# A gated hybrid decoder layer in split fp32: one planner orders everything from the second projection pass to w_o, the pooled branch moves ahead of the gates, five column pairs there use seven-product blocks, and convolution taps alternate between two tiles

## The chip, the core and the metric

The kernel runs on one core of a Trainium2 chip. The metric is the device time of one execution in microseconds (us). Three runs of the kernel before gave 1199.72, 1199.89 and 1200.82 us; their median is 1199.89.

Engines: TensorE (PE, with PEld for its weight loads) multiplies, VectorE (DVE) and ScalarE (ACT) do elementwise work, GpSimd (POOL) and SyncE (SP) here mostly start DMAs.

## The reference

272 tokens (16 meta tokens and a sequence of 256) of width 2048, one layer:

```python
u = rms_norm(h, g_pre_mix)
z_pool, v_conv, g_conv, gate_a, gate_b = split(u @ w_in)      # 1024 | 1024 | 1024 | 2048 | 2048
y_a = causal_multiscale_pool(z_pool, w_pool_grp, pool_scale) @ w_pool_out
y_b = conformer_conv(v_conv, g_conv, w_dw, b_dw, ...) @ w_conv_out
m = sigmoid(gate_a) * y_a + sigmoid(gate_b) * y_b
h = h + rms_norm(m @ w_o, g_post_mix)
h = h + rms_norm(square(relu(rms_norm(h, g_pre_mlp) @ w_up)) @ w_down, g_post_mlp)
return h[:, 16:]
```

The pool takes trailing means over 2, 4, 8 and 16 tokens in four channel groups, subtracts the token, and maps each group by a 256x256 matrix. The convolution multiplies v by sigmoid(g), applies 31 causal taps per channel, a LayerNorm over channels and a swish. Everything is fp32.

## The kernel before

**Split weights.** Each fp32 factor of a product is held as two fp32r parts, hi (rounded) and lo (the rest), and a product is three matmuls: hi·hi, lo·hi and hi·lo. Weights come in chunks of 128x2048 fp32 (1 MB), loaded by SP into one of three buffers `raw`. `open_chunk` (L300) makes the load and two instructions: ACT copies raw to hi (L319), DVE subtracts, lo = raw − hi (L322). Hi and lo each have three rooms in turn, so the split of a chunk can start when the chunk three places earlier has been multiplied. `fetch` (L339) hands out a chunk and issues the split of the one two ahead.

**Stages, in PE's order.** The first convolution pass v0; then g0, v1, g1, v2, g2, v3, g3 and z0 to z3, each a projection of 256 columns with features on partitions and 272 tokens in the free dimension (`project`, matmuls L497); 16 blocks of 512 columns for the two gates (`project_t`, matmuls L753, output tokens x columns; a chunk of 512 input features makes a product of 12 matmuls for each of the two token tiles, 2.72 us each, and a block has four chunks); the pool's group map (`acc_grp`, L497); w_pool_out (`acc_po`), w_conv_out (`acc_co`) and w_o (`acc_o`), four blocks each; and the MLP.

**What orders the other engines there.** Emission is in program order, and each engine runs its instructions in that order. `project` and `project_t` emit a matmul group, then take a given amount of small work (`fill`, in us of DVE) from a list `pending` by `drain`. The list holds the 240 convolution taps (`conv_tile`, L559 to L567: c = a·tap + c on 128x256, one channel tile after the other, 30 in a row for a tile, DVE L563), the pool's running sums (L673 to L685), and the LayerNorm steps (L698 to L731). Evacuations stand between them: L570, L577, L650 for the projections, L854, L882, L883 for the branches.

**The planner.** The MLP part of the kernel is ordered by a class `Plan` (L32 to L163). Each piece of work is added with its engine, a cost and what it reads and writes. PE's row is fixed by hand; each other piece gets a due time from the PE piece that needs it; a small simulation with the costs then always takes the ready piece that is due first, and the resulting start times give the order of emission. In the MLP the planner also orders "seven-product blocks": a 2x2x2 block product (two chunks of features by two column blocks by two token tiles) is done with seven products instead of eight, from sums of weight blocks and of activation blocks ("forms"). A weight sum is either a DVE addition on raw chunks (L1211), or a second load that POOL starts and that accumulates into the raw chunk (L1216).

Of the kernel before, what the change touches and what calls it, by code (L numbers as in the profile page):

```python
# [16 lines left out]
P = 128  # L17
CK = 4
# [12 lines left out]

class Plan:  # L32
# [5 lines left out]
    def __init__(self):  # L38
        self.work = []
        self.writer = {}  # L40
        self.readers = {}

    def add(self, engine, cost, f, reads=(), writes=(), late=0.0):
        i = len(self.work)
        before = set()
        for b in reads:
            if b in self.writer:
                before.add(self.writer[b])
        for b in writes:
            before.update(self.readers.get(b, ()))  # L50
            if b in self.writer:
                before.add(self.writer[b])
        for b in reads:
            self.readers.setdefault(b, []).append(i)
        for b in writes:
            self.writer[b] = i
            self.readers[b] = []
        before.discard(i)
        self.work.append((engine, cost, f, sorted(before), late))
# [107 lines left out]
def hybrid_block(ctx: ExitStack, tc: tile.TileContext, ins: dict, out: bass.AP):  # L167
# [88 lines left out]
    for h in range(CC // HALF_CW):  # L256
        for c0 in (PW, PW + CC):
            stream += columns(w_in, 0, KD, c0 + h * HALF_CW, HALF)
    for h in range(PW // HALF_CW):
        stream += columns(w_in, 0, KD, h * HALF_CW, HALF)  # L260
    standing_chunks = set()
    for n in range(2 * D // CW):
        stream += columns(w_in, 0, KD, G0 + n * CW)
    stream.append((w_grp.rearrange("g (k p) c -> p (g k) c", p=P), (NG * GD // P, GD)))
    for w, nk in ((w_pool_out, KP), (w_conv_out, KC)):
        for n in range(NB):
            stream += columns(w, 0, nk, n * CW)
    for n in range(NB):
        stream += columns(w_o, 0, KD, n * CW)

    spare = {len(stream) + 1: "s0", len(stream) + 2: "s1"}
    PF = 2 * CW
    NP = FF // PF
    standing_chunks.update(range(len(stream), len(stream) + NB + 2))
    stream += columns(w_up, 0, KD, 0)
    stream += columns(w_up, 0, KD, CW, HALF)
    FIRST = KD // HALF[0]
    opened = []
    at = {"n": 0}
# [3 lines left out]
    PLACES = {n: (2, 1) for n in standing_chunks}  # L283
# [16 lines left out]
    def open_chunk():  # L300
        n = at["n"]
        at["n"] += 1
        src, (rows, width) = stream[n]
# [4 lines left out]
        else:  # L308
            hi, lo = part_tile("hi", n), part_tile("lo", n)
# [158 lines left out]
    def scale_roots():  # L468
        tot = tmp.tile([P, NT + 1], F32, tag="tot", name="tot0")
        nc.vector.reduce_sum(tot, ssq, axis=mybir.AxisListType.X)  # L470
        nc.vector.tensor_scalar(tot, tot, 1.0 / D, RMS_EPS, op0=ALU.mult, op1=ALU.add)
        sc["r"] = r = const.tile([P, NT + 1], F32, name="r_in")
        q = tmp.tile([P, NT + 1], F32, tag="rs", bufs=1, name="rs_q_in")
        nc.scalar.activation(q, tot, AF.Sqrt)
        warm_up(AF.Sigmoid)
        rsqrt(r, q, tot)
        sc["diag"] = []
        for t in range(NT + 1):
            n = P if t < NT else M
            dg = tmp.tile([P, P], F32, tag="v", bufs=5, name=f"diag_{t}")  # L480
            nc.vector.tensor_scalar_mul(dg[:n, :n], ident[:n, :n], r[:n, t:t + 1])
            sc["diag"].append(dg)

    def scale_rows():
        pb = misc_tile("pb")
        for t, lo_, n in [(NT, 0, M)] + [(t, M + t * P, P) for t in range(NT)]:
            nc.tensor.matmul(pb[:, lo_:lo_ + n], ones[:n, :], sc["diag"][t][:n, :n],
                             start=True, stop=True)
        nc.vector.tensor_copy(rb, pb[:, :L])


# [28 lines left out]
    def project(act, nk, evac, name, mm=mm2, width=CW, shape=HALF, fill=0.0):  # L520

        ck, cw = shape
        accs = [acc[:, :width] for acc in acc_tiles(name, cw // P)]
        for kc in range(nk // ck):
            hi, lo = fetch()
            for j, acc in enumerate(accs):
                for k in range(ck):
                    kk = kc * ck + k
                    mm(acc, hi, lo, act, (k, kk), slice(j * P, (j + 1) * P), kk == 0, kk == nk - 1)
                if kc == nk // ck - 1:  # L530
                    flush(1)
                    evac(j, acc)
                if fill:
                    drain(fill * P / cw)

    def halves(acc, name):

        t = tmp.tile([P, T], F32, tag="v", bufs=5, name=f"half_{name}")
        nc.scalar.copy(t, acc[:, :T])
        s = tmp.tile([P, T], F32, tag="v", bufs=5, name=f"sum_{name}")  # L540
        nc.vector.tensor_add(s, t, acc[:, T:])
        return s

    def split(dst, k, src):
        def f():
            nc.scalar.copy(dst[:, k, 0, :], src)
            nc.vector.tensor_sub(dst[:, k, 1, :], src, f32(dst[:, k, 0, :]))
        late.append(f)


# [3 lines left out]

    def conv_tile(q):
        def first():
            nc.scalar.activation(conv["c"][:, q, :], conv["a"][:, q, 0:T], AF.Identity,
                                 scale=taps[:, q, 0:1], bias=col("b_dw", q))

        def tap(i):  # L560
            def f():
                c = conv["c"][:, q, :]
                nc.vector.scalar_tensor_tensor(c, conv["a"][:, q, i:i + T], taps[:, q, i:i + 1],  # L563
                                               c, op0=ALU.mult, op1=ALU.add)
            return f
        return [(0, first)] + [(0.39, tap(i)) for i in range(1, TAPS)]

    def evac_v(j, acc):
        v = tmp.tile([P, L], F32, tag="v", bufs=5, name=f"v_{j}")
        nc.vector.tensor_mul(v, acc[:, :L], rb)  # L570
        gv.append(v)

    def evac_g(j0):
        def f(j, acc):
            q = j0 + j
            g = tmp.tile([P, L], F32, tag="g", name=f"g_{q}")
            nc.vector.tensor_mul(g, acc[:, :L], rb)  # L577

            def gated():
                nc.scalar.activation(g, g, AF.Sigmoid)  # L580
                nc.vector.tensor_mul(conv["a"][:, q, PAD:], gv.pop(0), g)
                pending.extend(conv_tile(q))
            late.append(gated)
        return f

# [11 lines left out]
    accs = [acc[:, :L] for acc in acc_tiles("v0", HALF_CW // P)]  # L597
# [15 lines left out]
    def after_first():  # L613
        scale_rows()
        for j, acc in enumerate(accs):
            evac_v(j, acc)

    def tap_columns():
        rows_to_columns(*other_rows)
        pt = misc_tile("taps_t")  # L620
        for q in range(KC):
            nc.tensor.transpose(pt[:, q * 32:q * 32 + TAPS], taps_in[:, q * P:(q + 1) * P],
                                ident[:TAPS, :TAPS])
# [1000 lines left out]
```

## Time and profile before

| | |
|---|---|
| three runs | 1199.72, 1199.89, 1200.82 us |
| the profiled execution | 1200.3 us, of which 1198.5 us is the span from the first to the last instruction |
| granted TensorE clock, mean | 0.997 |
| busy in the span | PE 99%, PEld 86%, DVE 85%, ACT 55%, POOL 3% |
| DMA | 270.80 MB, 226 GB/s on average |

How to read it: "busy" is the time in which an engine runs instructions. PE's matmuls overlap, so the mean of one matmul in a list (390 ns) is longer than the distance from one to the next. A row of the view by windows gives, for a stretch of the span, the busy time of PE, PEld, DVE, ACT and POOL with the count of instructions in brackets, then the granted clock, the DMA share and GB/s. In this execution v0 ends and g0 begins at about 28.8 us, the gates run from 161 to 336, the group map to 342.6, w_pool_out to 386, w_conv_out to about 437, w_o to about 520 and the MLP to 1187.

### The profile page before, as it was taken

Reading aid. Unit: us, or ns where it says so; the run is one execution under the profiler, and the core shown is the slowest. Engines: PE = TensorE matmul, PEld = TensorE weight load, DVE = VectorE, ACT = ScalarE, POOL = GpSimd, SP = SyncE. Lnnn points to the kernel's source line nnn. Section 1 sums busy time; section 2 is a strip of 40 time slices with the busy share of each in tenths; the row PEclk is TensorE's granted clock in tenths of the full one; section 3 lists DMA queues with packets and bytes.
Section 4 is the critical chain, followed back from the end, with each engine's and each line's share of the span. In section 5 each row is a group of like instructions: output and inputs, shape, how many; then the busy total and the mean of one; then the engine's idle time right before and its main releaser. Section 6 shows DMA issues by size and latency. Waiting matters only on the chain.

```text
span 1198.5 us, 15727 instructions
## 1 busy us (share of the span) xinstructions
PE 1184.1 (99%) x6384; PEld 1026.1 (86%) x6384; DVE 1013.4 (85%) x1084; ACT 661.4 (55%) x664; POOL 41.7 (3%) x45
## 2 busy tenths in 40 slices
PE   9999999999999999999999999999999999999996
PEld 8999988888888888898888888888888888888885
DVE  5799987999767664577989999999999999899856
ACT  6633334434475334357676665666665756666542
POOL 1000000000000000000100000000000000000000
PEclk9999999999999999999999999999999999999998
DMA  8655555656556756549998897997997987979941
GB/s 257 210 178 180 179 191 187 198 189 201 185 176 212 280 176 201 186 123 354 245 332 231 236 314 203 243 319 189 289 293 199 309 236 240 316 179 263 332 139 71
DMA packets 176698, 270.80 MB, mean 226 GB/s; under 512 B 4482, under 2 KB 91970, under 8 KB 175713
## 3 DMA queue, kind: packets, MB, share of 16 engines
q1 hardware_dynamic: 160064, 235.09, 58.6%
q0 software_dynamic: 15408, 32.66, 15.1%
q10 hardware_dynamic: 1152, 2.04, 0.5%
q8 instruction: 50, 0.82, 0.3%
q14 instruction: 24, 0.19, 0.0%
HBM read 265.58 MB, written 4.19 MB: 225 GB/s over the span
## 4 chain that ended last, share of the span: by engine, by line
PE 98%; DMA 1%; DVE 1%; ACT 0%; ACTq 0%; issue 0%; DVEq 0%
PE bank_u L502 18%; PE acc_gate L753 15%; PE acc_up L1373 13%; PE bank_u L508 9%; PE bank_a L1373 7%; PE bank_b L1373 5%; PE acc_o L753 5%; PE acc_v L497 4%; PE acc_z L497 4%; PE acc_g L497 4%; PE acc_co L753 4%; PE acc_po L753 4%; PE acc_o_last L753 2%; PE acc_up L502 1%; PE bank_u L1373 1%; DMA x_in<-in_x_dram 1%
## 5 line engine op out<-in xcount | busy, mean ns | idle before, releaser
L502 PE MATMUL bank_u<-m,hi 128*128 128x512 f32 x960 | 329.4, 390 | 0.0
L319 ACT CAST hi<-raw 128x2048 fp32r<-128x2048 f32 (+1 forms) x114 | 180.8, 1594 | 228.6 <-PE acc_gate L753 71.5
L322 DVE TENSOR_TENSOR lo<-raw,hi 128x2048 fp32r<-128x2048 f32 (+1 forms) x114 | 215.4, 1896 | 76.0 <-ACT hi L319 75.6
L508 PE MATMUL bank_u<-m,lo 128*128 128x256 f32 x960 | 265.3, 276 | 0.0
L502 PEld LDWEIGHTS bank_u<-m,hi 128*128 128x128 f32 x960 | 180.2, 188 | 37.8
L508 PEld LDWEIGHTS bank_u<-m,lo 128*128 128x128 f32 x960 | 180.2, 188 | 1.6
L1199 DVE TENSOR_TENSOR lo<-raw_m,hi 128x2048 fp32r<-128x2048 f32 x71 | 162.4, 2288 | 15.1 <-ACT hi L1194 14.9
L1194 ACT CAST hi<-raw_m 128x2048 fp32r<-128x2048 f32 x71 | 135.8, 1913 | 51.6 <-PE bank_u L502 18.0
L753 PE MATMUL acc_gate<-hi,u_um 128*128 128x512 f32 x512 | 158.6, 390 | 0.0
L1373 PE MATMUL acc_up<-hi,forms 128*128 128x512 f32 x440 | 143.1, 390 | 0.7 <-ACT G L1398 0.7
L563 DVE SCALAR_TENSOR_TENSOR c<-a,taps,c 128x256 f32<-128x256 f32 x240 | 115.5, 484 | 6.6
L1199 DVE TENSOR_TENSOR lo<-raw_h,hi 128x2048 fp32r<-128x2048 f32 x46 | 105.2, 2287 | 12.8 <-ACT hi L1194 12.7
L1194 ACT CAST hi<-raw_h 128x2048 fp32r<-128x2048 f32 x46 | 88.0, 1913 | 50.5 <-PE bank_u L502 32.5
L753 PEld LDWEIGHTS acc_gate<-hi,u_um 128*128 128x128 f32 x512 | 96.1, 188 | 19.9
L753 PE MATMUL acc_gate<-lo,u_um 128*128 128x512 f32 x256 | 99.6, 389 | 0.0
L1373 PEld LDWEIGHTS acc_up<-hi,forms 128*128 128x128 f32 x440 | 82.6, 188 | 18.8 <-ACT G L1398 1.1
L1373 PE MATMUL acc_up<-lo,forms 128*128 128x512 f32 x220 | 85.9, 391 | 0.0
L1373 PE MATMUL bank_a<-hi,forms 128*128 128x512 f32 (+1 forms) x256 | 82.0, 383 | 0.0
L1373 PE MATMUL bank_b<-hi,forms 128*128 128x512 f32 (+1 forms) x200 | 63.4, 381 | 0.0
L1194 ACT CAST hi<-raw_a 128x2048 fp32r<-128x2048 f32 x23 | 44.0, 1912 | 34.0 <-PE bank_u L502 25.1
L1199 DVE TENSOR_TENSOR lo<-raw_a,hi 128x2048 fp32r<-128x2048 f32 x23 | 52.6, 2288 | 11.4 <-ACT hi L1194 11.3
L753 PE MATMUL acc_o<-hi,m 128*128 128x512 f32 x192 | 59.6, 390 | 0.0
(288 smaller groups left out, 1928.3 us busy)
## 6 DMA issues: line engine op xcount, KB each, us to landing
raw<-in_w_in_dram SPq DMA_DIRECT2D x54, 1024.0 KB, 5.2
raw_m<-in_w_up_dram SPq DMA_DIRECT2D x25, 1024.0 KB, 9.8
raw_m<-in_w_down_dram SPq DMA_DIRECT2D x22, 1024.0 KB, 7.8
raw_h<-in_w_down_dram SPq DMA_DIRECT2D x21, 1024.0 KB, 7.2
raw<-in_w_o_dram SPq DMA_DIRECT2D x16, 1024.0 KB, 5.2
raw_h<-in_w_up_dram SPq DMA_DIRECT2D x16, 1024.0 KB, 8.8
raw_a<-in_w_down_dram SPq DMA_DIRECT2D x12, 1024.0 KB, 5.9
raw_a<-in_w_up_dram SPq DMA_DIRECT2D x11, 1024.0 KB, 7.3
```

Of the source, the lines that this page charges most:

```text
L319: nc.scalar.copy(hi[:, sl, :], raw[:, sl, :])
L322: nc.vector.tensor_sub(lo[:, sl, :], raw[:, sl, :], f32(hi[:, sl, :]))
L497: nc.tensor.matmul(acc, w[:, k[0], cs], act[:, k[1], a, off:], start=first and n == 0, stop=last and n == 2)
L502: nc.tensor.matmul(acc.rearrange("p (a t) -> p a t", a=2)[:, :, ts], hi[:, k[0], cs], act[:, k[1], :, off + ts.start:off + ts.stop], start ...
L508: nc.tensor.matmul(acc[:, :T], lo[:, k[0], cs], act[:, k[1], 0, off:], start=False, stop=stop, skip_group_check=True)
L563: nc.vector.scalar_tensor_tensor(c, conv["a"][:, q, i:i + T], taps[:, q, i:i + 1], c, op0=ALU.mult, op1=ALU.add)
L753: nc.tensor.matmul(acc, act(kk)(a_, ts_), w_[:, k, :], start=kk == 0 and n == 0, stop=kk == nk - 1 and n == 2)
L1194: nc.scalar.copy(box["flat"], raw_in(room))
L1199: nc.vector.tensor_sub(lo, raw_in(room), f32(box["flat"]))
L1373: nc.tensor.matmul(acc, forms[h][:, f, k, a_, :], box[w_][:, k, cs], start=start and k == 0 and n == 0, stop=stop and k == KH - 1 and n == ...
```

## The change

Everything from g0 to w_o is now added to one `Plan`, and `project`, `project_t`, `fetch`, `pending` and `drain` are gone for that part. PE's row is written as data, `AFTER_G0` for the rest of the projections and a string `MAIN` for the rest:

```diff
-    project(u, KD, first_g, "g0", mm=mm3, width=L, fill=2.4)
-    for h in range(1, CC // HALF_CW):
-        project(u, KD, evac_v, f"v{h}", mm=mm3, width=L, fill=2.5)
-        project(u, KD, evac_g(h * HALF_CW // P), f"g{h}", mm=mm3, width=L, fill=2.4)
...
-        return [(0, first)] + [(0.39, tap(i)) for i in range(1, TAPS)]
...
+AFTER_G0 = [("z", 0), ("z", 1), ("z", 2), ("z", 3), ("v", 1), ("g", 1), ("v", 2), ("g", 2),
+            ("v", 3), ("g", 3)]
+MAIN = (
+    "fu p00 p01 p11 p21 p31 p10 p20 p30 k1 a0P1 a0P5 a12 a13 a0P6 a0P3 a2P1 a0P7 a0P2 a03 a0P4 "
+    "a2P5 a02 a33 a2P6 a2P3 a2P2 a2P7 a32 a22 b0P1 a23 a2P4 b0P5 b23 b13 b0P6 b12 b0P3 b22 b0P7 "
+    "b0P2 b03 b31 lnm b30 b0P4 lnv b20 b32 b02 b33 b21 um8 c01 c2P1 c00 c2P5 T00 c11 c10 c2P6 "
+    "c2P3 T11 T10 c2P2 c2P7 T01 o21 c2P4 T20 T31 o20 T21 T30 OF o22 o0P1 o0P5 o23 o13 o0P6 o0P3 "
+    "o0P7 o03 o02 o12 o0P4 o0P2 o30 o31 o32 o33 ")
+SUMMED = {"gate0": "56", "gate1": "56", "co": "56", "o": "56", "po": "56"}
...
+            if what == "sum":
+                plan.add("DVE", 2.22, lambda a=at_rooms[0], b=at_rooms[1]: nc.vector.tensor_add(
+                    rooms[a](), rooms[a](), rooms[b]()), reads=names, writes=names[:1], late=0.13)
+            elif what == "bring":
+                src, (rows, _) = source(extra)
+                plan.add("POOL", 5.9, lambda a=at_rooms[0], src=src, rows=rows: nc.gpsimd.dma_start(
+                    rooms[a]().rearrange("p (k c) -> p k c", k=rows), src, accum_op=ALU.add),
+                    reads=names, writes=names)
+            else:
+                high, low = split_of(w, at_rooms[0], source(raws_[0])[1][0])
+                h_, l_ = half_names(w)
+                plan.add("ACT", 1.82, high, reads=names, writes=(h_,), late=0.13)
+                plan.add("DVE", 2.22, low, reads=names + [h_], writes=(l_,), late=0.13)
...
+        def tap(i):
+            def f():
+                for q in on(q0, nq):
+                    nc.vector.scalar_tensor_tensor(
+                        C_c()[:, q, :], A_a()[:, q, i:i + T], taps[:, q, i:i + 1], C_c()[:, q, :],
+                        op0=ALU.mult, op1=ALU.add)
+            return f
+        for i in range(1, TAPS):
+            plan.add("DVE", 0.4 * nq, tap(i), reads=[f"a{q}" for q in on(q0, nq)],
+                     writes=[f"c{q}" for q in on(q0, nq)], late=0.1)
...
+        def give(self, s, bank):
+            n = self.n0
+            t, j = {"1": (0, 0), "5": (1, 1), "6": (0, 1), "7": (1, 1)}[s]
+            name, dst = self.place(t, n + j)
+            if s == "7":
+                on_vector(CW, lambda: nc.vector.tensor_sub(dst(), dst(), banks[bank]),
+                          (bank, name), (name,))
+                self.last_parts(name, dst)
+            else:
+                on_scalar(CW, lambda: nc.scalar.copy(dst(), banks[bank]), (bank,), (name,))
```

In `MAIN`, p is w_pool_out, a and b the two gates, c w_conv_out, o w_o. "a12" is the chunk of features 1 and column block 2 of gate a, done for both token tiles (24 matmuls). "a0P6" is product 6 of the seven-product block on column blocks 0 and 1 and feature chunks 0 and 1 (12 matmuls). T are transposes, fu and OF make the forms of activations, lnm and lnv are the LayerNorm's two sums. Part by part:

- **The pooled branch.** z0 to z3 come right after g0, then v1 to g3; the group map and w_pool_out follow, and the gates come behind them (before: gates, then group map and w_pool_out). Its result is copied by ACT to a buffer (L1135) and multiplied by the sigmoid when that is there (L1130).
- **Seven-product blocks** on gate a columns 0-1 and 2-3, gate b columns 0-1, w_conv_out columns 2-3 and w_o columns 0-1, each on the first two feature chunks. Products 5 and 6 use a weight sum made by DVE (L771), products 7 and 4 one brought by an accumulating load of POOL (L775). Partial results are kept by ACT copies (L1212) and put together by DVE (L1188, L1190, L1208).
- **Forms**, the sums and differences of activation blocks with their hi and lo parts (L1083 to L1095 for the gates; `make_forms` for w_conv_out and w_o).
- **Taps.** `convolve` (L877 to L892) emits tap i for both channel tiles of a pass before tap i+1.
- **Rooms.** Seven further places for raw chunks, used at different times, beside the three of before. Hi and lo keep three rooms in turn.
- **The planner's class** gets `take` (a new name takes over a room) and leaves out waits of PE on PE.

The whole program's instructions: PE matmuls on 128x512 go from 3856 to 3796, the others stay. DVE goes from 1086 to 1162: 25 more additions or subtractions on 128x2048 (15 splits, 10 sums), 46 more on 512 elements per partition, 6 more on 256, one less on 1024. ACT goes from 636 to 690 (15 more 2048-wide casts, 39 more copies of 512). POOL starts 10 more DMAs of 1 MB. SP starts 237 as before.

DVE's row in the pass v2 of the kernel before (L322 is a split, L570 and L577 evacuate, L563 is a tap; c, a and taps are the convolution's output, input and coefficients):

```order
L581 TENSOR_TENSOR a<-v_655,g_803 128x272
L581 TENSOR_TENSOR a<-v_703,g_832 128x272
L563 SCALAR_TENSOR_TENSOR c<-a,taps,c 128x256 x6
L322 TENSOR_TENSOR lo_905<-raw_903,hi_904 128x2048
L570 TENSOR_TENSOR v_933<-acc_v_0_837,rb 128x272
L563 SCALAR_TENSOR_TENSOR c<-a,taps,c 128x256 x4
```

DVE's row in the pass v3 of the kernel after (L759 is a split, L886 a tap, L864 and L870 evacuate, L874 makes a, L993 adds up the mean):

```order
L874 TENSOR_TENSOR a<-v_420,g_680 128x272
L886 SCALAR_TENSOR_TENSOR c<-a,taps,c 128x256 x8
L759 TENSOR_TENSOR lo_1692<-raw_s0a,hi_1686 128x2048
L864 TENSOR_TENSOR v_421<-bank_k_410,rb 128x272
L886 SCALAR_TENSOR_TENSOR c<-a,taps,c 128x256 x4
L864 TENSOR_TENSOR v_422<-bank_k_411,rb 128x272
L886 SCALAR_TENSOR_TENSOR c<-a,taps,c 128x256 x4
```

The six taps in a row of before belong to one channel tile; the eight of after are four taps of each of two tiles, one of each in turn.

DVE's row in the gates, which follow the projections in the kernel before:

```order
L322 TENSOR_TENSOR lo_2527<-raw_2525,hi_2526 128x2048
L563 SCALAR_TENSOR_TENSOR c<-a,taps,c 128x256 x6
L322 TENSOR_TENSOR lo_2563<-raw_2561,hi_2562 128x2048
L563 SCALAR_TENSOR_TENSOR c<-a,taps,c 128x256 x7
L322 TENSOR_TENSOR lo_2602<-raw_2600,hi_2601 128x2048
```

DVE's row after w_pool_out in the kernel after, where the first seven-product block begins. lo_2175, lo_2228, lo_2250 and lo_2308 are the splits for a0P1, a0P5, a12 and a13, lo_2342 and lo_2326 those for a0P6 and a0P3; L771 is a weight sum:

```order
L759 TENSOR_TENSOR lo_2175<-raw_p_418,hi_2168 128x2048
L886 SCALAR_TENSOR_TENSOR c<-a,taps,c 128x256 x2
L771 TENSOR_TENSOR raw_p_418<-raw_p_418,raw_p_416 128x2048
L886 SCALAR_TENSOR_TENSOR c<-a,taps,c 128x256 x6
L759 TENSOR_TENSOR lo_2228<-raw_p_418,hi_2208 128x2048
L886 SCALAR_TENSOR_TENSOR c<-a,taps,c 128x256 x2
L759 TENSOR_TENSOR lo_2250<-raw_p_417,hi_2244 128x2048
L886 SCALAR_TENSOR_TENSOR c<-a,taps,c 128x256 x14
L759 TENSOR_TENSOR lo_2308<-raw_k_2242,hi_2290 128x2048
L771 TENSOR_TENSOR raw_p_418<-raw_p_418,raw_k_2242 128x2048
L759 TENSOR_TENSOR lo_2326<-raw_k_2242,hi_2310 128x2048
L759 TENSOR_TENSOR lo_2342<-raw_p_418,hi_2328 128x2048
```

Between two splits, where taps alone stood, there are now also the sums, and the last four 2048-wide instructions stand directly one behind the other. The same place on ACT in the kernel after (L754 is the copy to hi, L1135 and L1212 put away results of w_pool_out and of the block):

```order
L1135 COPY ya<-bank_k_411 128x512
L1212 COPY sg_2264<-bank_k_412 128x512
L1212 COPY sg_2264<-bank_k_413 128x512
L754 CAST hi_2290<-raw_k_2242 128x2048
L754 CAST hi_2310<-raw_k_2242 128x2048
L754 CAST hi_2328<-raw_p_418 128x2048
L754 CAST hi_2345<-raw_p_417 128x2048
```

The cast for a0P3 (hi_2310) stands ahead of the one for a0P6 (hi_2328), though PE multiplies a0P6 first.

More of the change, by code (lines that the diff above doesn't have):

```diff
@@ L57, in add @@
             self.readers[b] = []
+        if engine == "PE":
+            before = {b for b in before if self.work[b][0] != "PE"}
         before.discard(i)
@@ new lines, in hybrid_block @@
+    steps[3:3] = [("rows",), ("taps",)]
+    steps += [("close", 5), ("close", 6), ("grp", "grp", 0, 0)]
+    STAGE = {"p": "po", "a": "gate0", "b": "gate1", "c": "co", "o": "o"}
+    for word in MAIN.split():
+        if word[0] not in STAGE:
+            steps.append(("T", int(word[1]), int(word[2])) if word[0] == "T" else (word,))
+        elif word[2] == "P":
+            steps.append(("S", STAGE[word[0]], int(word[1]), word[2:]))
+        else:
+            steps.append(("N", STAGE[word[0]], int(word[1]), int(word[2])))
@@ L993, in hybrid_block @@
     assert NT == 2 and NB == 4 and CK == 4
[L994 to L995 removed]
+    two = [opened.pop(0)[:2] for _ in range(2)]
     while len(opened) < 3:
```

1014 lines of the change are left out of this document (704 added, 310 removed).

## The prediction

> **What bounds the kernel now.** I read first the page's shares of busy time, then its chain of work that ended last.
>
> ```profile
> PE 1184.1 (99%) x6384; PEld 1026.1 (86%) x6384; DVE 1013.4 (85%) x1084; ACT 661.4 (55%) x664; POOL 41.7 (3%) x45
> PE 98%; DMA 1%; DVE 1%; ACT 0%; ACTq 0%; issue 0%; DVEq 0%
> ```
>
> PE is busy 1184.1 of 1198.5 us, and the chain is 98% PE. So a matmul less is worth its whole distance to the next, as long as every other engine keeps pace; and the other engines can only cost time. Where could they? The view by windows (columns after the two times: PE, PEld, DVE, ACT, POOL, clock, DMA share, GB/s) cuts the span by stages; the last three rows are the MLP's start, its seven-product blocks, and the tail.
>
> ```profile
> 28.80:161.00 132.20, 132.20 (x1073) 131.79 (x1072) 117.62 (x180) 55.45 (x55) 0.19 (x1) 1.00 0.58 184
> 161.00:336.00 175.00, 175.00 (x773) 144.65 (x772) 154.00 (x194) 78.45 (x60) 0.00 (x0) 1.00 0.59 192
> 336.00:345.00 9.00, 8.55 (x61) 7.90 (x60) 5.47 (x9) 7.96 (x12) 0.00 (x0) 1.00 0.69 228
> 345.00:386.00 41.00, 41.00 (x183) 33.96 (x182) 29.44 (x21) 25.27 (x28) 0.00 (x0) 1.00 0.54 181
> 386.00:432.00 46.00, 46.00 (x217) 38.36 (x216) 30.76 (x28) 18.22 (x14) 1.28 (x2) 1.00 0.72 251
> 432.00:500.00 68.00, 68.00 (x306) 56.40 (x305) 35.13 (x26) 28.38 (x27) 0.00 (x0) 1.00 0.58 190
> 545.00:600.00 55.00, 54.31 (x295) 46.61 (x294) 50.09 (x55) 41.39 (x58) 3.88 (x3) 1.00 0.99 294
> 600.00:1140.00 540.00, 540.00 (x2801) 462.84 (x2800) 505.86 (x424) 343.07 (x290) 32.06 (x25) 1.00 0.91 263
> 1187.00:1198.50 11.50, 0.23 (x2) 0.03 (x1) 6.47 (x15) 0.71 (x3) 0.00 (x0) 0.65 0.49 183
> ```
>
> In the region of the change, 28.8 to 500, PE idles once, for 0.45 us, in the window of the group map. VectorE is the next engine: 117.6 + 154.0 + 5.5 + 29.4 + 30.8 + 35.1 = 372 us of 471. One row here carries much of my belief: for 540 us of the MLP, a planner keeps PE without idle time while DVE is busy 505.9 (94%), ACT 64%, DMA 91%, with seven-product blocks and loads that POOL starts. A DVE filled that far can be hidden here.
>
> **What the blocks remove.** The chain lists PE's pieces without a gap, with start, length and count.
>
> ```profile
> 28.81 11.84 PE acc_g L497 x96
> 342.74 43.55 PE acc_po L753 x192
> 438.82 59.85 PE acc_o L753 x264
> ```
>
> 59.85 / 264 = 0.2267 us for a matmul of 128x512 from one start to the next; w_pool_out gives the same. Each of the five blocks saves one product of eight, 12 matmuls: 60 x 0.2267 = **13.6 us less PE**. The passes of 272 columns (11.84 us each) and the group map only move. The clock stays at 1.00 in every working window, so nothing is to be had there.
>
> **What that costs VectorE.** These rows give the price of each instruction; the first two are groups by shape, the third a weight sum of the MLP, the others stretches of DVE's timeline (start, length, count).
>
> ```profile
> L322 DVE TENSOR_TENSOR lo<-raw,hi 128x2048 fp32r<-128x2048 f32 x90 | 206.0, 2290 | 75.7 <-ACT hi L319 75.3
> L563 DVE SCALAR_TENSOR_TENSOR c<-a,taps,c 128x256 f32<-128x256 f32 x240 | 115.5, 484 | 6.6
> L1211 DVE TENSOR_TENSOR raw_m<-raw_m,raw_h 128x2048 f32<-128x2048 f32 x6 | 13.7, 2284 | 0.0
> ...
> 151.43 2.29 DVE L322 TENSOR_TENSOR lo<-raw,hi 128x2048 fp32r<-128x2048 f32 x1
> 153.63 3.09 DVE L563 SCALAR_TENSOR_TENSOR c<-a,taps,c 128x256 f32<-128x256 f32 x6
> ...
> 171.93 0.69 DVE L685 TENSOR_TENSOR d<-dm,d 128x512 fp32r<-128x512 f32 x1
> 172.53 0.71 DVE L673 TENSOR_TENSOR sums<-sums 128x538 f32<-128x538 f32 x1
> ```
>
> A 2048-wide instruction lasts 2.29 but the next one starts after 153.63 − 151.43 = 2.20; a weight sum costs as much as a split. A 512-wide one takes 172.53 − 171.93 = 0.60 to the next. Added: 25 x 2.20 + 46 x 0.60 + 6 x 0.35 = 55.0 + 27.6 + 2.1 = **85 us** (0.35 is my estimate for 256 wide, in proportion between these two).
>
> **What the taps give back.** Six taps of one tile last 3.09 us: (3.09 − 0.484) / 5 = 0.52 from start to start, longer than the 0.484 of one. Eight instructions of the same operation and width that do not use one another, the group map's evacuations, stand here, and beside them PE's one wait:
>
> ```profile
> 340.51 3.26 DVE L816 SCALAR_TENSOR_TENSOR y<-acc_grp,vecs,y 128x256 fp32r<-128x256 f32 x8
> ...
> 341.04 0.50 PE L497 MATMUL acc_grp<-d,hi 128*128 128x256 f32 x2 [0.45 <-DVE y L816]
> ```
>
> (3.26 − 0.476) / 7 = 0.40 from start to start, with 0.476 the duration of one in the view by groups:
>
> ```profile
> L816 DVE SCALAR_TENSOR_TENSOR y<-acc_grp,vecs,y 128x256 fp32r<-128x256 f32 x8 | 3.3, 476 | 0.0
> ```
>
> So an instruction that waits for the one right ahead of it pays 0.12 us. In the program of before 185 of the 240 taps do so; in the new order none does, since the tap of the other tile stands between. Saving: 185 x 0.12 = **22 us**. The trace has no instruction that depends on the second one ahead, so this is bounded: by 22 us if distance two is enough, by nothing if it is not. I take 22, because two steps of 0.40 are 0.80 us, well over the 0.52 that a result needs.
>
> The Trainium skill, page "VectorE: DVE Perf Modes", section "The DRAIN you can't avoid", speaks against this edit: the next operation does not start until the pipe is empty, and chaining without semaphores gains nothing. By that rule the alternation would save nothing and the sum below would lose these 22 us. The two rows above disagree with it: 0.40 us is less than the 0.476 that one such instruction lasts.
>
> Net: DVE +85 − 22 = +63 us, so 372 + 63 = 435 us in 471 − 14 = 457 us of PE, **95%**. That is the MLP's figure, but not evenly spread. Piece by piece:
>
> **Projections.** Half a pass (5.92 us of PE, half of 11.84) now holds on DVE a split, two evacuations of 0.36 and eight taps: 2.2 + 0.7 + 3.2 = 6.1 us; the neighbouring half has one small instruction less, about 5.75. So DVE is full there, and stays so in w_pool_out: a split and eight taps, 5.4 us, to a chunk of 43.55 / 8 = 5.44. It works at its limit from about 50 to 290 us, and any lateness is carried along, not made good. It isn't late at first, since the three hi/lo rooms let a split start early and the planner gives splits due dates ahead of taps.
>
> **First seven-product block.** Here the three rooms decide. From the end of g3's first half, which frees the room for w_pool_out's first chunk, PE needs 5.9 + 5.8 (group map, 48 matmuls at about 0.12, since 11.84 / 96 = 0.123 with 272 columns) + 43.6 + 16.3 (a0P1, a0P5, a12, a13, 72 matmuls) = 71.6 us to a0P6. DVE, from the end of that chunk's split, has in its row 13 splits, two sums, eight evacuations of the group map, 78 taps, four instructions for the forms and four evacuations: 15 x 2.2 + 8 x 0.40 + 78 x 0.40 + 4 x 0.60 + 4 x 0.35 = 71.2 us. It can't begin before that first split is done, 1.91 for ACT's cast and 2.29 after the room is free, 4.3 with the hand-over. 4.3 + 71.2 − 71.6: PE waits **3.9 us**, in one piece or, in part, already at the group map, whose evacuations stand behind a split again (0.45 before; now part of the 3.9). Behind a0P6 on PE stands everything else, so the whole wait reaches the end.
>
> The cast's duration:
>
> ```profile
> L319 ACT CAST hi<-raw 128x2048 fp32r<-128x2048 f32 x90 | 171.9, 1912 | 228.6 <-PE acc_gate L753 71.5 <-PE acc_o L753 26.4 <-issue 24.3
> ```
>
> From below: if DVE were ahead, the room alone would give a product of 2.72 us its split 1.91 + 2.29 after the product three earlier; with a0P3's cast ahead of a0P6's that still costs between 0 and 1 us. From above: DVE a further 1% slower over 235 us adds 2.4, and a second wait of equal kind in the next block 4. I take 3.9 and half of that 1%, **5 us**, with 0 and 10 as ends.
>
> **Later blocks.** From a0P6 on, summed by the same prices, DVE's row to each further split is no longer than PE's: by half a microsecond at the closest, in the first two blocks, by 3 us at the end of the gates and by 10 behind them. So nothing more accrues unless the prices are low. A copy or an addition that puts a partial result away holds one of six banks. ACT, busy 40 to 62% in these windows, gets 15 x 1.91 + 39 x 0.5 (a quarter of the cast, an estimate) = 48 us more in 457; hidden. Were its cover gone, it would be the split that waits, as above.
>
> **Loads.** Ten loads by POOL are added, SP's stay 237. Their price, issue to landing, stands on the page.
>
> ```profile
> raw_m<-in_w_down_dram POOLq DMA_DIRECT2D x11, 1024.0 KB, 9.5
> raw<-in_w_in_dram SPq DMA_DIRECT2D x54, 1024.0 KB, 5.2
> ```
>
> A brought sum needs 9.5 + 4.2 for its split, 13.7 us. The shortest distance in PE's row is from product 6 to product 4 of w_conv_out's block, 16 us; 19 for the first block. The region's DMA share is 0.54 to 0.72, and 10 MB more leave room; behind such a load stand on POOL only the next one and the loads of h1 and of the gain, wanted much later. Nothing on the path; at twice 9.5 us each block would lose about 4.
>
> **The sum.** Profiled execution 1200.3 (span 1198.5 and 1.8 around it, 0.4 over the median 1199.89): 1200.3 − 13.6 − 0.45 + 5 = **1191.2**; against the median 1190.8. I forecast 1191. The waits' ends, 0 and 10, give 1186 and 1196. The MLP and the tail of 11.5 us stay.
>
> **The rivals.**
>
> *All hidden.* The planner holds DVE ahead, PE waits for nothing: 1186. For it speaks the MLP, 94% without a wait; against it that the MLP's load is even, and here 100% for 240 us is followed at once by short products.
>
> *VectorE becomes the bound.* Distance two is not enough and the taps stay at 0.52: DVE then has 240 x 0.12 = 29 us more than I counted, of which slack before the projections are full and behind the gates takes about 6. PE waits 5 + 23: 1214, slower. The point from which it decides: with 5 us already waited, 9 us more use up the gain; 9 / 240 = 0.04, so a tap spacing of 0.44. Against it: 0.40 in the row of independent instructions. The skill's rule on the DRAIN, above, would make this the outcome.
>
> *Waits across the blocks.* Casts behind copies, room for raw chunks, and brought loads at twice 9.5 us cost 2 to 3 us in each block: 13 us of waits, 1199, no change. For it: every block has five 2.72 us products close together, and ACT's and DVE's orders come from costs, not from times. Against it: the same construction in the MLP idles 0 in 540 us with a DMA share of 0.91.
>
> **How the numbers follow.** A measurement of this kernel can tell about 0.2%, 2.4 us, from no change. Forecast (1188 to 1196) 0.56; all hidden (1185.5 to 1188) 0.15; waits across the blocks (1196 to 1201) 0.14; VectorE bound (1204 to 1216) 0.15. The range 1185.5 to 1200 holds the first two and most of the third, 0.82. Faster by over 0.2% (below 1197.5): 0.56 + 0.15 + 0.08 = 0.79; within 0.2%: 0.06; slower: 0.15.
>
> **What the profile after would show.** PE's matmuls of 512 at 0.227 still, 60 fewer. Taps in turn at 0.40 a piece: if 0.52, the second rival holds. DVE near 95% from 29 to about 490, and nearly 100% in v, g and w_pool_out. PE's idle time in the region some 5 us, most of it at the first block, released by DVE splits; if it is released by DMA or ACT, or lies in the blocks of gate b, w_conv_out or w_o, the third rival is the right one. I am wrong if PE's idle there is above 10 or below 2.

## The result and the profile after

Five runs of the kernel after gave 1194.31 to 1195.61 us, median **1194.93**; five of the kernel before on the same chip 1199.72 to 1200.88, median 1200.34. The ratio is 0.9955, 95% interval 0.994 to 0.9969: faster by 0.45%. The forecast was 1191, the range 1185.5 to 1200. The profiled execution took 1194.8 us, its span 1193.0, against 1200.3 and 1198.5.

(A correction to the section on the change: in `MAIN` the word "a12" names column block 1 and feature chunk 2, not the reverse. No number hangs on it.)

The page of the kernel after, busy time and the chain that ended last:

```profile
PE 1172.1 (98%) x6324; PEld 1013.9 (85%) x6324; DVE 1076.1 (90%) x1160; ACT 710.4 (60%) x718; POOL 54.6 (5%) x55
PE 78%; DVE 9%; DMA 7%; ACT 4%; issue 1%; ACTq 0%; DVEq 0%; SPq 0%
```

VectorE is 62.7 us busier (63 forecast). The chain, 98% PE before, now passes through VectorE, DMA and ScalarE for a fifth of the span. PE's waits in the region of the change, from its timeline (start, length, the instruction, then the idle time ahead of it and who ended it):

```profile
48.03 0.26 PE L837 MATMUL bank_y<-ident,rows_pool_scale 48*128 48x48 f32 x1 [0.53 <-DVE rb L828]
166.73 0.50 PE L490 MATMUL acc_v<-d,hi 128*128 128x256 f32 x2 [0.84 <-DVE y L983]
218.08 0.50 PE L1166 MATMUL bank_k<-hi,u_um 128*128 128x512 f32 x1 [0.68 <-ACT sg L1212]
225.54 0.50 PE L1166 MATMUL bank_k<-lo,u_um 128*128 128x512 f32 x1 [1.49 <-DVE lo L759]
232.15 0.50 PE L1166 MATMUL bank_k<-lo,forms_k 128*128 128x512 f32 x1 [0.87 <-DVE lo L759]
304.04 0.50 PE L1166 MATMUL bank_k<-lo,u_um 128*128 128x512 f32 x1 [0.88 <-DVE lo L759]
425.68 0.50 PE L1166 MATMUL bank_k<-lo,m 128*128 128x512 f32 x1 [1.57 <-DVE lo L759]
```

Seven waits, 6.86 us, where one of 0.45 was. In order: the transposes of the convolution's vectors, the group map, a12, a13 and a0P6 of the first block, gate b, w_o. Each costs about 0.16 us more than its idle time, the hand-over: the matmul ahead of a wait is counted as busy for its 0.39 us, where without the wait the next one would have started after 0.227. (An estimate; the 0.39 and 0.227 are those of 512 columns.) Together 6.86 + 7 x 0.16 = 8.0 us, against 0.6 before. The account: −13.6 + 8.0 − 0.6 = −6.2; the profile has −5.5. A wait in the MLP that is 0.3 longer and one at the first tile 0.2 longer explain part, a tail 0.35 shorter works against it; about 0.5 us is not located.

VectorE by stretches of the span (PE, PEld, DVE, ACT, POOL, clock, DMA share, GB/s), kernel after:

```profile
28.80:100.00 71.20, 70.67 (x574) 70.21 (x574) 62.40 (x98) 35.10 (x39) 0.19 (x1) 1.00 0.63 205
100.00:161.00 61.00, 61.00 (x497) 61.00 (x496) 60.41 (x102) 23.78 (x20) 0.00 (x0) 1.00 0.48 156
161.00:212.00 51.00, 50.16 (x246) 42.44 (x245) 51.00 (x85) 27.63 (x31) 1.37 (x1) 1.00 0.45 146
212.00:260.00 48.00, 44.96 (x196) 36.24 (x195) 46.47 (x47) 27.39 (x20) 2.57 (x2) 1.00 0.96 277
260.00:300.00 40.00, 40.00 (x178) 33.14 (x177) 38.65 (x42) 23.89 (x18) 2.56 (x2) 1.00 0.82 243
300.00:340.00 40.00, 39.12 (x172) 32.03 (x172) 40.00 (x49) 23.11 (x16) 1.28 (x1) 1.00 0.82 263
```

From 100 to 212 us DVE is busy 111.4 of 112 us, and PE waits 0.84 there: full, and just in time. In the gates it is at 97 to 100%. What it lacks there stands in two places, each ahead of waits of PE for a split (ACT and DVE before a13's split, then the same two at 278 us; the last line is the chain's, the load that the second pair waits for):

```profile
221.25 1.91 ACT L754 CAST hi<-raw_k 128x2048 fp32r<-128x2048 f32 x1 [3.22 <-DMA raw_k<-in_w_in_dram]
223.20 2.29 DVE L759 TENSOR_TENSOR lo<-raw_k,hi 128x2048 fp32r<-128x2048 f32 x1 [1.27 <-ACT hi L754]
...
277.81 1.91 ACT L754 CAST hi<-raw_p 128x2048 fp32r<-128x2048 f32 x1 [2.84 <-DMA raw_p<-in_w_in_dram]
279.75 2.29 DVE L759 TENSOR_TENSOR lo<-raw_p,hi 128x2048 fp32r<-128x2048 f32 x1 [1.35 <-ACT hi L754]
...
268.05 9.66 DMA raw_p<-in_w_in_dram
```

So VectorE itself stood still 1.27 and 1.35 us there, for a cast that waited for a load.

### The profile page after: what moved, and what is told of

It is laid out like the page before. It is cut to its first block, busy times and chain, and to the rows that moved or that the text cites. A ratio compares the mean times of both kernels' runs of the same rounds, so it can differ in the third digit from the quotient of the medians.

```text
span 1193.0 us, 15777 instructions
## 1 busy us (share of the span) xinstructions
PE 1172.1 (98%) x6324; PEld 1013.9 (85%) x6324; DVE 1076.1 (90%) x1160; ACT 710.4 (60%) x718; POOL 54.6 (5%) x55
## 4 chain that ended last, share of the span: by engine, by line
PE 78%; DVE 9%; DMA 7%; ACT 4%; issue 1%; ACTq 0%; DVEq 0%; SPq 0%
PE bank_u L495 16%; PE acc_up L1850 12%; PE bank_k L1166 11%; PE bank_u L501 8%; PE bank_k L490 7%; PE bank_a L1850 7%; PE bank_b L1850 5%; PE acc_v L490 4%; DVE lo L759 4%; PE acc_v L1166 4%; ACT hi L754 2%; DMA raw_p<-in_w_in_dram 2%; DMA kept<-h 1%; DVE c L886 1%; DVE raw_p L771 1%
## 5 line engine op out<-in xcount | busy, mean ns | idle before, releaser
L754 ACT CAST hi<-raw_p 128x2048 fp32r<-128x2048 f32 x66 | 125.9, 1912 | 107.9 <-PE bank_k L1166 28.2
L759 DVE TENSOR_TENSOR lo<-raw_p,hi 128x2048 fp32r<-128x2048 f32 x66 | 150.4, 2287 | 15.6 <-ACT hi L754 15.4
L886 DVE SCALAR_TENSOR_TENSOR c<-a,taps,c 128x256 f32<-128x256 f32 x240 | 100.6, 480 | 0.2
L490 PE MATMUL bank_k<-u_um,hi 128*128 128x272 f32 x512 | 95.0, 287 | 0.0
L1166 PE MATMUL bank_k<-hi,u_um 128*128 128x512 f32 x272 | 87.2, 391 | 0.7 <-ACT sg L1212 0.7
L490 PEld LDWEIGHTS bank_k<-u_um,hi 128*128 128x128 f32 x512 | 79.9, 188 | 0.0
L490 PE MATMUL bank_k<-u_um,lo 128*128 128x272 f32 x256 | 73.3, 286 | 0.0
```

Source lines behind the costliest of these rows:

```text
L490: nc.tensor.matmul(acc, w[:, k[0], cs], act[:, k[1], a, off:], start=first and n == 0, stop=last and n == 2)
L754: nc.scalar.copy(box["flat"], rooms[q]())
L759: nc.vector.tensor_sub(lo, rooms[q](), f32(box["flat"]))
L886: nc.vector.scalar_tensor_tensor(C_c()[:, q, :], A_a()[:, q, i:i + T], taps[:, q, i:i + 1], C_c()[:, q, :], op0=ALU.mult, op1=ALU.add)
L1166: nc.tensor.matmul(banks[bank], a_(k, part), box[w_][:, k, :], start=opens and k == 0 and i == 0, stop=ends_ and k == CK - 1 and i == 2, s ...
```

## The experiments

**Theory.** The gain is the 60 matmuls, and only they; VectorE, at its limit up to the LayerNorm, turns whatever it loses into PE waits. **Rivals.** The new order has a worth of its own; or the waits come from transfers, not from VectorE. Each ratio below is to executions of the kernel before in the same round; their medians were 1200.26 to 1200.34 us.

| run | median, us | ratio to before, 95% interval |
|---|---|---|
| after | 1194.93 | 0.9955 (0.994 to 0.9969) |
| e1, taps by tile, priced 0.52 | 1216.33 | 1.0131 (1.0117 to 1.0145) |
| e2, no blocks | 1203.95 | 1.0029 (1.0018 to 1.004) |
| e9, no blocks, taps by tile | 1203.08 | 1.0027 (1.0016 to 1.0037) |
| e3, before with alternating taps | 1200.15 | 0.9998 (0.9989 to 1.0007) |
| e4, first block plain, one product twice | 1196.91 | 0.9972 (0.9961 to 0.9982) |
| e5, product 6's sum brought | 1223.53 | 1.0195 (1.0181 to 1.0209) |
| e6, second load later | 1195.69 | 0.9965 (0.9953 to 0.9978) |
| e7, e5 and e6 | 1224.41 | 1.0187 (1.0174 to 1.0201) |
| f1, first block plain | 1193.77 | 0.9946 (0.9932 to 0.9959) |
| f2, f1 and product 4's sum by DVE | 1193.94 | 0.9951 (0.9938 to 0.9963) |
| g1, brought load held back | 1196.35 | 0.9969 (0.9958 to 0.998) |
| g2, g1 and product 4's sum by DVE | 1200.15 | 0.9996 (0.9984 to 1.0007) |

**e3: the taps alone, in the kernel before.**

```diff
-                pending.extend(conv_tile(q))
+                pair.append(conv_tile(q))
+                if len(pair) == 2:
+                    pending.extend(item for both in zip(*pair) for item in both)
+                    pair.clear()
```

> The kernel before, with the taps of the two tiles of a pass in turn and nothing else changed. Theory: PE waits only 0.45 us for VectorE in this region, so shorter taps change nothing: 1199 to 1201.5 us, with VectorE busy some 15 us less and taps 0.40 us apart. Rival (VectorE already cost time that the chain does not show): 1197 us or less.

1200.15, no change. A line of the view by groups and one of DVE's timeline in this run:

```profile
L564 DVE SCALAR_TENSOR_TENSOR c<-a,taps,c 128x256 f32<-128x256 f32 x240 | 99.0, 478 | 0.3 <-ACT c L558 0.3
...
153.62 2.46 DVE L564 SCALAR_TENSOR_TENSOR c<-a,taps,c 128x256 f32<-128x256 f32 x6
```

Six taps last 2.46 instead of 3.09 us: (2.46 − 0.478) / 5 = 0.396 a tap. So one instruction in between is enough, as forecast, and VectorE's 14.4 us less of busy time (1013.4 to 999.0) buy nothing while its work is hidden.

**e2 and e9: no seven-product blocks.**

```diff
-    "... k1 a0P1 a0P5 a12 a13 a0P6 a0P3 a2P1 ... "
+    "... k1 a00 a01 a02 a03 a10 a11 a12 a13 a20 ... b22 lnm b23 b30 lnv b31 b32 b33 um8 c00 c01 ... "
```

> The kernel after, all stages with plain products (no seven-product blocks); one plan, pooled branch ahead of the gates and alternating taps stay. Theory: the whole gain is the 60 matmuls, order and taps alone give nothing: 13.6 us more PE, waits down to 1 to 2 us, 1200 to 1202.5 us, the same as the kernel before. Rival (the new order or the planner has a gain of its own and the blocks give less): below 1198 us.

> As the run without blocks, and the taps of one tile in a row. Theory: without the blocks VectorE has 85 us less to do, taps at 0.52 us are hidden as in the kernel before: within 1.5 us of the run without blocks, 1200 to 1203.5 us. Rival (the new order itself crowds VectorE, since pool sums, taps and evacuations now stand in a shorter stretch): 1205 us or more.

1203.95 and 1203.08: the plan, the taps and an order of this kind without blocks gain nothing, they lose some 3 us. The rival falls, as far as this order stands for the one of the kernel after. e2's time lies 1.5 above what I expected; its profile has two waits of 2.05 us together at w_conv_out's start, which my order of the products makes: it leaves only three products between the second LayerNorm sum and that stage, where the kernel after has five. e9 says little of the taps: the planner again put taps of other tiles between those of one (see e1).

**e1: taps of one tile before those of the other.**

```diff
-        for i in range(1, TAPS):
-            plan.add("DVE", 0.4 * nq, tap(i), reads=[f"a{q}" for q in on(q0, nq)],
-                     writes=[f"c{q}" for q in on(q0, nq)], late=0.1)
+        for q in on(q0, nq):
+            for i in range(1, TAPS):
...
+                plan.add("DVE", 0.52, one, reads=[f"a{q}"] + [f"c{p}" for p in on(q0, q - q0)],
+                         writes=[f"c{q}"], late=0.1)
```

> The kernel after, with the 30 taps of one tile in a row before the other tile's (the planner is given 0.52 us a tap). Theory: VectorE is at its limit from the projections to the gates, so what the taps cost more comes out as PE waits. Taps at 0.52 us from start to start, VectorE about 25 us busier than after up to the end of the gates, PE idle in the region 20 to 30 us instead of 7, time 1208 to 1218 us, slower than the kernel before. Rival (the planner hides the taps wherever they stand, VectorE is not the limit): 1194 to 1197 us.

1216.33, inside the range, but not for the reason given. PE's long waits and a stretch of DVE's timeline:

```profile
353.37 0.80 PE L1171 MATMUL bank_k<-hi,u_um 128*128 128x512 f32 x1 [8.10 <-DVE sg L1193]
362.89 1.22 PE L1010 MATMUL bank_y<-v,ones 128*128 128x256 f32 x2 [4.34 <-DVE v L998]
...
342.34 10.37 DVE L893 SCALAR_TENSOR_TENSOR c<-a,taps,c 128x256 f32<-128x256 f32 x26
```

(10.37 − 0.48) / 25 = 0.396: these taps were not slower. So it is with nearly all strings of taps in e1, six of them have the 0.52; the planner must have mixed the tiles of several passes. What changed is the price it was told. The same windows of DVE as above, in e1:

```profile
28.80:100.00 71.20, 70.67 (x573) 70.21 (x573) 59.75 (x87) 35.87 (x41) 0.19 (x1) 1.00 0.65 206
100.00:161.00 61.00, 61.00 (x497) 61.00 (x496) 55.57 (x88) 23.28 (x19) 0.00 (x0) 1.00 0.47 155
161.00:212.00 51.00, 50.64 (x249) 42.91 (x249) 46.90 (x71) 27.27 (x31) 1.37 (x1) 1.00 0.46 148
212.00:260.00 48.00, 45.74 (x199) 36.87 (x199) 43.83 (x42) 27.73 (x21) 2.57 (x2) 1.00 0.98 281
260.00:300.00 40.00, 40.00 (x178) 33.12 (x177) 38.18 (x41) 25.59 (x19) 2.55 (x2) 1.00 0.83 245
300.00:340.00 40.00, 39.87 (x176) 32.67 (x175) 37.76 (x49) 20.85 (x14) 1.28 (x1) 1.00 0.79 254
```

Up to 340 us DVE has done 282.0 us of work against 298.9 in the kernel after: the planner, taking a tap for 0.52, put too few between two splits, and DVE idled. 17 us lost there come back as PE waits of 8.10 + 4.34 + 1.99 + 1.73 = 16.2 at the end of the gates. So VectorE has no slack before the LayerNorm, one microsecond lost is one paid. The time grew by 21.4 us: PE's idle time in the region is 14.2 longer than in the kernel after, and its busy time 6.7 (1178.8 against 1172.1), with a clock of 0.50 from 353 to 358 and from 362 to 368 us, behind the two longest waits. But that dependent taps at 0.52 would cost this is argued only: no run had them together with the blocks.

**e4 and f1: the first block by plain products.**

```diff
-    "... k1 a0P1 a0P5 a12 a13 a0P6 a0P3 a2P1 a0P7 a0P2 a03 a0P4 a2P5 a02 ... "
+    "... k1 a00 a01 a12 a13 a10 a11 a2P1 a03 a2P5 a02 ... "
```

> The kernel after without the first seven-product block (gate a, columns 0 and 1, by plain products), the other four stay. Theory: this block saves 2.7 us of PE and costs 3.0 us of waits at its own place (0.68 + 1.49 + 0.87 idle in the profile of after); without it VectorE has some 7 us less before the gates. PE idle near 218 to 232 us gone, time 1193.5 to 1196 us, the same as after. Rival (the waits come from the projections and move on to the next block): 1196.5 to 1198.5 us.

e4's order also had "a02" ahead of a03, so that column block 0's chunk 2 was counted twice; f1 is without that.

> The kernel after without the first seven-product block: gate a, columns 0 and 1, by plain products, each done once; the other four blocks stay. (The run e4 did one of these products twice, 24 matmuls or 5.4 us more PE, and gave 1196.9, so about 1191.5 without that.) Theory: the first block costs more in waits (0.68 + 1.49 + 0.87 at its place, 0.88 at 304 us, each with 0.16 of hand-over) than its 2.7 us of PE: 1190.5 to 1193 us, faster than after. Rival (the block pays, its waits move on to the next one): 1194 to 1197 us.

f1 took 1193.77. The waits at 218 to 232 us are gone (PE is busy 42.00 of 42 us from 210 to 252), the 2.7 us of PE come back. Its interval and that of the kernel after overlap: the first block is worth nothing either way, within about two microseconds. I expected more, since I took e4's second a02 for its full 5.4 us of PE; it cost 3.1 (1196.9 against 1193.8). In the profiled executions the MLP begins at 514.1 us in f1 and at 518.0 in e4, 3.9 apart, for e4 has 1.0 us less of PE waits (2.35 against 3.34) and two hand-overs fewer; f1's MLP then lasts 2.0 us longer, which is not explained. The block costs about what it saves.

**e5, e6, e7: the splits of the first block.**

```diff
-SUMMED = {"gate0": "56", "gate1": "56", ...
+SUMMED = {"gate0": "5", "gate1": "5", ...
```

> The kernel after with the weight sum for product 6 of the three gate blocks brought by an accumulating load of POOL, not added by VectorE: three 2048-wide additions less on VectorE, three loads of 1 MB more. Theory (VectorE's rate sets the waits at 232 and 304 us): those two, 1.75 us together, go, the wait for a13's load stays; 1192.5 to 1194.5 us. Rival (transfers at the start of the gates are what is late): the three loads slow the others, a13's load takes over 9 us, 1195.5 to 1199 us.

1223.53, on the rival's side and far beyond its range. PE's waits in the gates:

```profile
239.76 0.70 PE L1166 MATMUL bank_k<-hi,forms_k 128*128 128x512 f32 x1 [3.79 <-ACT hi L754]
244.32 0.79 PE L1166 MATMUL bank_k<-lo,forms_k 128*128 128x512 f32 x1 [3.86 <-DVE lo L759]
...
286.30 0.50 PE L1166 MATMUL acc_v<-hi,forms_k 128*128 128x512 f32 x1 [3.83 <-ACT hi L754]
292.17 0.80 PE L1166 MATMUL acc_v<-lo,forms_k 128*128 128x512 f32 x1 [5.37 <-DVE lo L759]
```

Product 6's sum lies on top of product 5's, so its load starts only when that is split: in the first block at 213.13 us, behind another brought load of 208.84, and it landed 15.0 us later. a13's load, issued at 211.43, took 12.12 us (8.88 in the kernel after), and PE waited 2.61 and 1.83 for it. Behind a13 the casts for a0P3 and a0P6 stand one after the other from 236.01, and PE waits the 3.79 and 3.86 shown. Ahead of the waits in the second block, 3.83 and 5.37, the chain runs through splits and taps, not through a load; that the planner's price of 5.9 us for a brought load put them so late is argued, not shown. Three additions less, 6.6 us of VectorE by their price, cost 28.6 us.

e6 gave the second room for raw chunks free one product later (`plan.take(["raw3"], names_y + half_names(m_ - 1))` in a step behind a0P5).

> The kernel after; the second of the two loads that start when w_pool_out has read its last input (at 212.0 us, the chunk for product 3 and the sum of product 6) is issued behind the load that follows it, so that the chunk for a13 lands alone. Theory: a13 waits for its load (8.9 us for two at once) and not for VectorE: it lands in 5 to 6.5 us, the wait of 1.49 us at a13 shrinks below 0.5, that at a0P6 grows by up to 1: 1193.5 to 1195 us. Rival (VectorE alone sets the wait): a13's split at the same time as before, 1194.5 to 1196 us.

> Both of the last two edits: product 6's weight sum in the gates by a load, and the second load at 212 us later. If VectorE's rate and the load each carry a part, the gains add: 1192 to 1194 us. If transfers are the limit here, 1195.5 us or more.

1195.69 and 1224.41: e6 changed nothing, e7 is e5. In e6 the load for a13 still took 9.01 us, from 211.88, although SP's next load started only at 216.28. So what made it slow was not SP's next load.

**g1: POOL's load.** The chain of waits of the kernel after, from the end of w_pool_out to a13's split, and POOL's row for the load brought for product 7:

```profile
212.00 8.88 DMA raw_k<-in_w_in_dram
...
221.25 1.92 ACT hi L754
...
223.20 2.29 DVE lo L759
...
209.41 1.37 POOL L775 DMA_DIRECT2D raw_p<-in_w_in_dram  x1 [169.55 <-DVE c L886]
```

The room for a13's chunk comes free at 212.0, with w_pool_out's last product; the chunk lands 8.88 us later, and PE waits 1.49. g1 holds the brought load until it has landed:

```diff
+                if raws_[0] == ("gate0", 3, 1):
+                    plan.add("POOL", 0.2, lambda q=at_rooms[0]: nc.gpsimd.tensor_copy(
+                        warm, rooms[q]()[:, 0:1]), reads=names, writes=("dot",))
...
-                    reads=names, writes=names)
+                    reads=names + ["dot"] * (raws_[0] == ("gate0", 0, 1)), writes=names)
```

> The kernel after, with the brought load for product 7 of the first block held back by a one-column copy on POOL that reads the chunk for a13, so that a13's load has the DMA engines alone. Theory: a13's load, which can start only at 212 us, takes 8.9 us because that brought load runs beside it; alone it takes 5.2 to 6.5, the wait of 1.49 at a13 falls below 0.4 and a0P6's (0.87) does not grow by more than 0.5; 1193 to 1194.3 us. Rival (VectorE's rate): the wait moves to a0P6, the sum of both stays above 2 us, 1194.5 to 1196 us.

The chain of g1 at the same place:

```profile
211.84 5.34 DMA raw_k<-in_w_in_dram
...
217.26 1.90 ACT hi L754
219.16 0.49 ACT sg L1215
...
219.70 4.45 PE bank_k L1169 x12
```

The load takes **5.34 us instead of 8.88**, and the waits at a13 and a0P6 are gone, both of them. Yet the time is 1196.35, above both ranges: a13's chunk now lands just when product 5 ends, ACT casts it first (1.90), and a12 waits 2.45 us (0.68 before) for the copy that frees its bank; product 7's own sum, 14 us later than before, now stands close to the next brought load, a plain load issued at 231.22 takes 11.45 us, and new waits of 0.92 and 0.85 come at 247 and 276 us. The rate of all transfers in 40 slices of the stretch from 205 to 222 us, first the kernel after, then g1:

```profile
GB/s 10 0 0 0 0 0 0 0 0 0 0 0 0 0 39 92 120 145 164 212 202 207 212 212 207 207 246 284 251 313 357 400 410 390 419 405 410 414 390 390
```

```profile
GB/s 0 0 0 0 0 0 0 0 0 0 0 0 0 0 39 0 0 0 82 63 140 357 410 405 410 419 395 405 395 400 390 386 371 386 376 395 381 381 337 87
```

From 213 to 216 us the kernel after moves some 207 GB/s; g1 moves some 400 from 214 us on. Whose bytes are they? The queues of the kernel after from 212 to 216 us (packets, MB, share of 16 engines); q0 is POOL's, 528 packets for a brought load of 1 MB, q1 is SP's:

```profile
q0 software_dynamic: 372, 0.76, 106.6%
q1 hardware_dynamic: 2, 0.00, 0.3%
```

So the plain load, issued at 212.00, gets no share: nearly every packet until 216 is the brought load's, and a13's chunk comes only when most of that has passed.

**f2 and g2: the wait in w_o.** There the load for the waiting product was issued at 412.22, behind a load that POOL had started at 410.28, and took 9.09 us; from then to 416 us all 323 packets are POOL's. Both runs let VectorE make that sum (`"co": "564"`).

> As f1, and the weight sum for product 4 of w_conv_out's block added by VectorE, not brought by POOL at 410 us. Theory: the wait in w_o (1.57 us in after, 0.98 in e4) is for a load that takes 9.1 us beside that brought load and 5.2 alone; without it the wait is gone, 0.7 to 1.5 us less than f1, 1189.3 to 1192 us. Rival (VectorE's rate makes that wait; an addition more of 2.2 us makes it longer): f1's time or up to 2 us more.

> All five blocks, g1's held load and f2's sum by VectorE. Theory (waits at a13 and in w_o are loads that meet brought loads): both gains add, 1191.5 to 1193 us. It is to be compared with f2: if the first block pays once its load is in time, this one is not slower than f2. Rival (VectorE's rate): 1194 us or more.

In f2 that load takes 5.3 us (9.5 in f1) and the wait in w_o, 1.14 in f1, is gone; waits of 0.20, 0.50 and 0.47 at 417, 432 and 448 us, for VectorE and ScalarE, stand in its place: 1193.94, no gain. g2 took 1200.15, on the rival's side: with its load held, the first block costs more than it saves (f2, without it, is 6.2 us faster). Its profiled execution, 1198.8, has a12's wait (2.70), five small new ones around w_conv_out, and 3.3 us more of PE's busy time than the kernel after, with a clock of 0.50 behind a12's wait; why one execution reached 1204.5 stays open.

## Why the forecast was right, and where not

- **60 x 0.2267 us.** Right: 72 matmuls of w_pool_out, the shape of the blocks' too, take 16.35 us in the kernel after, 0.227 each, and e2 without the blocks is 9.0 us slower than the kernel after, which is 13.6 less the waits that the blocks bring.
- **VectorE +63, taps at 0.40.** The spacing is right, 0.396 in e3 and after. The 62.7 agrees in part by luck: e3 shows that the taps alone give back 14.4 us of busy time, not 22, since the rest were gaps that the view counts as idle; so the added work is 62.7 + 14.4 = 77 us, not 85, and the two errors cancel. That the alternation is what keeps the change fast is argued from 22 us and a full row, not shown. The Trainium skill's rule on the page "VectorE: DVE Perf Modes", section "The DRAIN you can't avoid", that the next operation waits for an empty pipe, disagrees with these 0.396 us: the instruction lasts 0.478, and the next one starts before it ends; the same section adds that a next operation that is not held starts earlier.
- **VectorE full from 50 to 290 us, lateness is carried.** Right from 100 to 212 us: 60.41 of 61 and 51.00 of 51, and e1's 17 us come back as 16.2. From 212 to 300 it is at 97%, and idles 1.27 and 1.35 us for loads.
- **Group map and first block 3.9 us.** The size is right, 0.84 + 0.68 + 1.49 + 0.87 = 3.88, mostly by luck. I gave all of it to VectorE's row, and only the 0.84 at the group map is that row alone. The 0.68 is for a copy on ScalarE that frees a bank. The 1.49 and the 0.87 come behind a load that stands behind a brought load; in g1, with that load in time, both are gone. But g1 also shows that a cast and a copy on ScalarE are then as late.
- **"Later blocks: nothing more accrues."** The step that failed, with the next one. 0.88 came at gate b. DVE is at 40.00 of 40 there, but the chain leads back to a load issued at 268.05, behind a brought load of 266.12, that took 9.66 us, and to the 1.35 us for which DVE then idled. No run moved that brought load, so this is read from the chain, not shown.
- **"Loads: nothing on the path."** Failed: I priced the brought load itself, 9.5 us, and not what it does to the plain load behind it, 9 us instead of 5.3. That made the 1.49 and 0.87 of the first block (g1), the 1.57 in w_o (f2), and by the chain the 0.88: 4.8 of 6.86 us. The third rival thus happened in part, at three places and smaller than I had put it; by the sign that I named for it, waits in gate b and w_o, the 0.88 and the 1.57 are its own.
- **The sum.** Waits with hand-over 8.0 instead of 5, and 0.5 not located: 1194.8 for the profiled execution instead of 1191.2. The time came out in the range because the matmuls were right and the waits happened to be of about the size forecast, most of them for another reason. The 0.53 at the transposes was not foreseen: the bank they use is still read by the copy of rb.

A version clearly faster than the kernel after was not found. f1, with four blocks, lies 1.2 us below it, inside both intervals.

## What to carry to other kernels

When an edit trades work of the bound engine for work of the next one, add up the second engine's row against the first's place by place, not by stage; where that row is full, a block can cost in waits what it saves, as the first one did here. Count a transfer twice, by its own time and by what it does to the load issued behind it. And a planner is only as good as its prices: one wrong by 0.12 us, 240 times, cost 21 us.

## What the hardware did that was not expected

An accumulating load of 1 MB halves what the DMA engines move, some 207 GB/s against some 400 without it, and holds up the plain loads issued 2 to 3 us behind it: in the rows of g1's section 372 of 374 packets in 4 us are its own. It is no strict order: in e5, with two brought loads close together, both queues move about as much from 220 to 224 us (0.53 and 0.51 MB).

PE's clock falls after shorter waits than I would have thought. The timeline and a window of g1 behind a12's wait of 2.45 us:

```profile
219.70 0.80 PE L1169 MATMUL bank_k<-hi,u_um 128*128 128x512 f32 x1 [2.45 <-ACT sg L1215]
220.29 0.63 PE L1169 MATMUL bank_k<-lo,u_um 128*128 128x512 f32 x1
...
219.80:221.00 1.20, 1.20 (x3) 1.01 (x4) 1.20 (x1) 0.00 (x0) 1.20 (x1) 0.50 1.05 384
222.00:223.00 1.00, 1.00 (x4) 0.82 (x3) 1.00 (x1) 0.00 (x0) 1.00 (x1) 0.59 0.08 31
```

For about 3 us matmuls run at half rate: the twelve of the chain's last line in g1 take 4.45 us instead of 2.72, 1.7 us on top of the wait. In g2 the same wait is 2.70 us, and the clock falls only when PE has worked again for about a microsecond (1.00 from 220 to 221 us, 0.61 in the next one, then 0.50). After the waits of 1.49 and 1.57 us in the kernel after and of 1.99 in e1 the clock stays at 1.00. The Trainium skill, page "TensorE: Matmul & The Clock Gate", section "Part 1: The HAM clock gate", gives an idle window of about 3.4 us for this; here 2.45 was enough.
